# Joining the 16-row inverses of RWKV's time mixing by 32 by 32 products in the array's own tiles

## The chip, the core and the metric

The kernel runs on one core of one Trainium2 chip. The metric is the device time of one execution in microseconds, as the median over several runs of the same program. A profile of one execution stands beside the times; its span runs from the first to the last instruction of the core.

## What is computed

Two layers over all 256 positions at once, everything in float32. Each layer is half a SwiGLU, a mixer, half a SwiGLU:

```python
x = x + 0.5 * swiglu(rms_norm(x, ffn1_norm[l]), ffn1_w_gate_up[l], ffn1_w_down[l])
u = rms_norm(x, mix_norm[l]) @ w_in[l]                 # split: SSD | mLSTM | RWKV-7
x = x + concat(y_ssd, y_mlstm, y_rwkv) @ w_out[l]
x = x + 0.5 * swiglu(rms_norm(x, ffn2_norm[l]), ffn2_w_gate_up[l], ffn2_w_down[l])
```

The change lies in the RWKV-7 part, which the reference writes as a recurrence over time for each of 8 heads of 64:

```python
def step(s, inp):
    r_t, w_t, k_t, v_t, kk_t, a_t = inp
    sa = einsum('bhvk,bhk->bhv', s, -kk_t)
    s = s * w_t + sa[..., None] * (kk_t * a_t) + v_t[..., None] * k_t
    return s, einsum('bhvk,bhk->bhv', s, r_t)
```

The kernel works in chunks of 64 positions. Inside a chunk the values `sa` of all positions solve a triangular system, (I + N) U = R, where N is strictly triangular, 64 by 64. There are 8 heads and 4 chunks, so 32 such matrices in a layer; the kernel needs their inverses.

## The kernel before

**The dense work.** The large products (gate/up, down, `w_in`, `w_out`) run as three passes of 32-bit-rounded matmuls, since every weight and activation is split into a high and a low part. A weight piece of 128 by 1024 numbers is loaded by SyncE's DMA queue (L742 to L766), split by ScalarE (L821) and VectorE (L822), and used by TensorE (L854 to L856 in `mm3`, L1070 and L1073 in `gate_up`).

**What sets the order.** Every operation is first recorded by a `Planner`. It has its own costs for each kind of instruction and for each engine's queue, and picks one instruction after the other: on TensorE the dense work fills what the mixers leave, and work that waits for another engine is put off by a margin as long as something else can go. It also places tiles in a shared store of 22 regions, so a smaller tile can let a weight piece be loaded earlier. Every engine then executes its own list strictly in that order. So a change of a few operations gives other lists on all engines.

**The inverse.** The four 16 by 16 diagonal blocks of each matrix go through DRAM (`dn`, L1333 and L1336) so that all 128 blocks lie one on a partition; VectorE inverts them by substitution (L1359 and L1361, 15 steps). They come back through DRAM (`dg`, `dh`, L1366 to L1375) as block diagonals: `G` holds the inverses and `H` their transposes (the kernel keeps both forms, since the array multiplies by a transpose). In both, row blocks 0 to 63 hold one chunk's matrices and rows 64 to 127 those of the other chunk, 16 matrices in each half, 64 columns each.

Two rounds of joining follow. The first takes the parts of N that join 16 to 32 (`M1`, copied out by L1346, with zeros elsewhere): one product Q of `M1` and `G`, then one of `H` and Q that is taken from `G` and one of Q and `H` that is taken from `H` (each multiplies by the transpose of its first factor). The second takes the parts that join 32 to 64, which stay in `NMv` after the diagonal 32 by 32 blocks have been overwritten with zeros by GpSimd (L1348): a product Q of that part and `G`, and one of Q and `H` that is taken from `H`. Each of these five products is one call of `all_pairs` (L1415): 16 matrices in each of two halves, 32 matmuls of 64 by 64 by 64 in two banks of 16 matmuls each, with the tiles at rows 0 and 64 in turn. Each bank is taken out by one ScalarE copy (L1432, L1441) or one VectorE subtraction (L1436, L1437, L1443) of 128 by 512.

After it, a serial loop over the four chunks (L1482 to L1508) uses `H`, with mLSTM's and SSD's matmuls (L1657, L1663, L1677, L1703, L1800) and dense ones put between its steps.

A float32 matmul of the program appears as two MATMUL rows in the trace, and as two weight loads.

## Time and profile before

| what | value |
|---|---|
| median of three runs | 1283.59 us (1280.87 to 1286.09) |
| the profiled execution | 1280.8 us, its span 1279.1 us |
| TensorE, matmul rows | 1236.7 us busy, 97% |
| VectorE | 894.2 us, 70% |
| ScalarE | 700.3 us, 55% |
| GpSimd | 91.7 us, 7% |
| L1423, the five products | 640 matmul rows in two layers |

The page's first part gives busy time, share of the span and count by engine. The view by windows gives the same for stretches of the span, and the timeline lists an engine's instructions in order, with the idle time before a row and what ended it in brackets. Rows of the same line that follow each other are merged: the first number is the start, the second the time from that start to the end of the last, and x32 the number of instructions. The ends of matmuls are modelled, so in a merged row the last matmul's own duration is to be taken off before the rest is divided among the starts.

### The profile page before, as it was taken

Reading aid. Unit: us, or ns where it says so; the run is one execution under the profiler, and the core shown is the slowest. Engines: PE = TensorE matmul, PEld = TensorE weight load, DVE = VectorE, ACT = ScalarE, POOL = GpSimd, SP = SyncE. Lnnn points to the kernel's source line nnn. Section 1 sums busy time; section 2 is a strip of 40 time slices with the busy share of each in tenths; the row PEclk is TensorE's granted clock in tenths of the full one; section 3 lists DMA queues with packets and bytes.
Section 4 is the critical chain, followed back from the end, with each engine's and each line's share of the span. In section 5 each row is a group of like instructions: output and inputs, shape, how many; then the busy total and the mean of one; then the engine's idle time right before and its main releaser. Section 6 shows DMA issues by size and latency. Waiting matters only on the chain. (4 is left out here: it accounts for less than half of the span.)

```text
span 1279.1 us, 21014 instructions
## 1 busy us (share of the span) xinstructions
PE 1236.7 (97%) x7938; PEld 1067.8 (83%) x7938; DVE 894.2 (70%) x1448; ACT 700.3 (55%) x1233; POOL 91.7 (7%) x153
## 2 busy tenths in 40 slices
PE   7999998989999999999999999999899999999997
PEld 6888887978997888888878888789889888888886
DVE  6766666876599476666676666769766993766664
ACT  7555545647456375555565555565575553655553
POOL 2000002210012010000000000121100220000001
PEclk9999999999999999999999999999999999999999
DMA  9986644035347596655556656610532675966300
GB/s 318 341 267 188 191 116 116 1 87 130 108 143 256 172 311 204 198 186 169 173 165 187 176 183 179 167 48 2 149 92 85 205 255 165 311 198 194 103 1 33
DMA packets 281877, 210.22 MB, mean 164 GB/s; under 512 B 23856, under 2 KB 257200, under 8 KB 281776
## 3 DMA queue, kind: packets, MB, share of 16 engines
q1 hardware_dynamic: 281776, 208.89, 53.9%
q8 instruction: 62, 1.02, 0.3%
q14 instruction: 39, 0.32, 0.1%
HBM read 207.01 MB, written 1.84 MB: 163 GB/s over the span
## 5 line engine op out<-in xcount | busy, mean ns | idle before, releaser
L822 DVE TENSOR_TENSOR region<-region,region 128x1024 fp32r<-128x1024 f32 (+1 forms) x382 | 445.2, 1209 | 76.6 <-ACT region L821 75.1
L1070 PE MATMUL bank<-region,region 128*128 128x512 f32 x1280 | 402.1, 395 | 0.0
L821 ACT ACTIVATE region<-region 128x1024 fp32r<-128x1024 f32 (+1 forms) x382 | 377.9, 1039 | 30.1 <-DMA region<-in_w_in_dram 7.8
L854 PE MATMUL bank<-region,region 128*128 128x512 f32 (+1 forms) x1104 | 385.9, 350 | 6.4 <-DVE region L1190 3.2
L856 PE MATMUL bank<-region,region 128*128 128x512 f32 (+1 forms) x1104 | 383.7, 349 | 3.4 <-DVE region L873 2.9
L855 PE MATMUL bank<-region,region 128*128 128x512 f32 (+1 forms) x1104 | 384.1, 348 | 0.0
L1073 PEld LDWEIGHTS bank<-region,region 128*128 128x128 f32 x1280 | 240.2, 188 | 55.3
L1073 PE MATMUL bank<-region,region 128*128 128x256 f32 x1280 | 252.9, 278 | 0.0
L854 PEld LDWEIGHTS bank<-region,region 128*128 128x128 f32 x1104 | 209.9, 190 | 31.5 <-DVE region L1190 2.6
L856 PEld LDWEIGHTS bank<-region,region 128*128 128x128 f32 x1104 | 209.7, 190 | 30.6 <-DVE region L873 3.8
L855 PEld LDWEIGHTS bank<-region,region 128*128 128x128 f32 x1104 | 210.0, 190 | 23.4 <-issue 1.7
L1070 PEld LDWEIGHTS bank<-region,region 128*128 128x128 f32 x1280 | 200.9, 189 | 6.6 <-DVE region L873 0.3
L1081 ACT ACTIVATE region<-bank 128x256 f32<-128x256 f32 (+1 forms) x84 | 31.0, 374 | 209.4 <-PE bank L1073 209.4
L1083 DVE TENSOR_TENSOR region<-bank,region 128x256 f32<-128x256 f32 (+1 forms) x84 | 34.3, 411 | 117.8 <-ACT region L1081 117.8
L1085 ACT ACTIVATE region<-region 128x256 f32<-128x256 f32 (+1 forms) x84 | 33.9, 407 | 55.8 <-DVE region L1084 55.8
L873 DVE TENSOR_TENSOR region<-region,region 128x256 fp32r<-128x256 f32 (+2 forms) x88 | 36.9, 424 | 37.0 <-ACT region L872 37.0
L872 ACT ACTIVATE region<-region 128x256 fp32r<-128x256 f32 (+2 forms) x88 | 36.2, 417 | 38.8 <-DVE region L1087 38.4
L890 POOL TENSOR_SCALAR smalls<-smalls 128x1 f32<-128x1 f32 x14 | 6.1, 434 | 623.7 <-ACT region L886 623.6
L886 ACT ACTIVATE region<-res 128x512 f32<-128x512 f32 x28 | 17.6, 630 | 53.4 <-DVE res L882 51.4
L1190 DVE SCALAR_TENSOR_TENSOR region<-bank,pv,region 128x255 f32<-128x255 f32 (+2 forms) x84 | 39.9, 479 | 4.7 <-ACT region L1187 2.6
L872 ACT ACTIVATE region<-bank 128x512 fp32r<-128x512 f32 x28 | 16.6, 599 | 41.3 <-PE bank L1202 20.3
L1087 DVE TENSOR_TENSOR region<-region 128x256 f32<-128x256 f32 (+1 forms) x70 | 28.7, 413 | 9.7 <-ACT region L1085 2.6
(303 smaller groups left out, 1026.0 us busy)
## 6 DMA issues: line engine op xcount, KB each, us to landing
region<-in_f_gu_dram SPq DMA_DIRECT2D x352, 256.0 KB, 4.7
region<-in_f_dn_dram SPq DMA_DIRECT2D x88, 512.0 KB, 5.4
region<-in_w_in_dram SPq DMA_DIRECT2D x80, 512.0 KB, 4.6
region<-in_w_out_dram SPq DMA_DIRECT2D x32, 512.0 KB, 4.7
region<-in_prow_dram SPq DMA_DIRECT2D x4, 512.0 KB, 4.3
region<-in_prow_dram SPq DMA_DIRECT2D x6, 256.0 KB, 4.4
region<-in_w_gate_dram SPq DMA_DIRECT2D x2, 512.0 KB, 3.7
dn<-region SPq DMA_DIRECT2D x64, 4.0 KB, 1.5
```

The source lines that it names most:

```text
L821: act.activation(out=hi[:, c], in_=src[:, c], func=AF.Copy)
L822: dve.tensor_tensor(out=lo[:, c], in0=src[:, c], in1=hi[:, c].bitcast(F32), op=ALU.subtract)
L854: pe.matmul(o, lhsT=ah, rhs=bh, start=start, stop=False, skip_group_check=True)
L855: pe.matmul(o, lhsT=ah, rhs=bl, start=False, stop=False, skip_group_check=True)
L856: pe.matmul(o, lhsT=al, rhs=bh, start=False, stop=stop, skip_group_check=True)
L872: act.activation(out=hi, in_=src, func=AF.Copy)
L873: dve.tensor_tensor(out=lo, in0=src, in1=hi.bitcast(F32), op=ALU.subtract)
L1070: pe.matmul(banks[g], lhsT=wh[:, k, g, :], rhs=hT.both(4 * i + k), start=i == k == 0, stop=False, skip_group_check=True)
L1073: pe.matmul(banks[g][:, T:], lhsT=wl[:, k, g, :], rhs=hT(4 * i + k)[0], start=False, stop=i == 1 and k == 3, skip_group_check=True)
L1083: dve.tensor_tensor(out=s[:, ts], in0=gate[:, ts], in1=s[:, ts], op=ALU.add)
L1085: act.activation(out=s[:, ts], in_=s[:, ts], func=AF.Silu)
L1190: dve.scalar_tensor_tensor(out=dst[:, s:T], in0=ps[:, 0:T - s], scalar=col(cw + 3 - s), in1=dst[:, s:T], op0=ALU.mult, op1=ALU.add)
```

## The change

The matrices are no longer kept as 64 by 64 with zeros. `G` now holds the 32 by 32 diagonal blocks alone (32 columns for each of 16 matrices, 512 in place of 1024); so do `M1` and a new `G_` for the transposes. `H` stays 64 wide, and only its lower-left 32 by 32 corner is zeroed.

The first round is three calls of `blocks`: each has 64 matmuls of 32 by 32 by 32, in the four tiles of the array at rows 0, 32, 64 and 96, all into one bank. VectorE subtracts once from `G` (128 by 512) and four times, 32 partitions at a time, into the diagonal blocks of `H`. The second round is two products of 32 matmuls each, only for the one 32 by 32 block that is not zero: the first reads rows 0 to 31 of a half and writes rows 32 to 63, the second goes back. ScalarE takes them out in two copies of 32 partitions each, and the last copy has the factor -1 and writes the corner of `H` that no other operation writes. Since `NMv`'s block is read directly, GpSimd's 8 memsets a layer on it are gone.

So 160 float32 matmuls a layer of 64 by 64 by 64 become 256 of 32 by 32 by 32. The DMAs are as many and as large as before. The loads of two rows of parameters (`lnw`, `lnb`, L1400 and L1401) are recorded as to follow `H`'s writes; `H` is now written by DMA no more, so they wait for its memset alone.

```diff
-            M1 = new(1024)
+            M1 = new(512)
...
-                        act.activation(out=M1n[rr, i * 4:i * 4 + 4, :, d + 16:d + 32],
+                        act.activation(out=M1n[rr, i * 4:i * 4 + 4, :, 16:32],
                                        in_=NMv[i][rr, :, c, :, c0 + d + 16:c0 + d + 32], func=AF.Copy, scale=rmask[rr])
-                        gps.memset(NMv[i][rr, :, c, :, c0 + d:c0 + d + 32], 0.0)
...
-            G, H = (new(1024).rearrange("p (n t) -> p n t", n=16) for i in range(2))
+            G, G_ = (new(512).rearrange("p (n t) -> p n t", n=16) for i in range(2))
+            H = new(1024).rearrange("p (n t) -> p n t", n=16)
             gps.memset(G, 0.0, after=pm)
-            gps.memset(H, 0.0, after=pm)
-            for dst, src in ((G, dg), (H, dh)):
+            gps.memset(G_, 0.0, after=pm)
+            for c in range(2):
+                gps.memset(H[64 * c + 32:64 * c + 64, :, 0:32], 0.0, after=pm)
+            for dst, src in ((G, dg), (G_, dh)):
...
-            def all_pairs(lhs, rhs):
-                for i in range(2):
-                    b = bank()
-                    bv = b.rearrange("p (n t) -> p n t", n=8)
-                    for n in range(8):
-                        for r0 in (0, 64):
-                            q = slice(r0, r0 + 64)
-                            pe.matmul(bv[q, n, :], lhsT=lhs(q, i * 8 + n), rhs=rhs(q, i * 8 + n),
-                                      start=True, stop=True)
-                    yield slice(i * 8, i * 8 + 8), bv
+            def blocks(lhs, rhs):
+                b = bank().rearrange("p (n t) -> p n t", n=16)
+                for n in range(16):
+                    for r0 in range(0, 128, 32):
+                        q = slice(r0, r0 + 32)
+                        pe.matmul(b[q, n, :], lhsT=lhs[q, n, :], rhs=rhs[q, n, :], start=True, stop=True)
+                return b
+            def kept(b, rows=(slice(0, 128),)):
+                v = new(512).rearrange("p (n t) -> p n t", n=16)
+                for q in rows:
+                    act.activation(out=v[q], in_=b[q], func=AF.Copy)
+                return v
...
+            Q = kept(blocks(M1v, G))
+            dG, dH = blocks(G_, Q), blocks(Q, G_)
+            dve.tensor_tensor(out=G, in0=G, in1=dG, op=ALU.subtract)
+            for r0 in range(0, 128, 32):
+                q = slice(r0, r0 + 32)
+                c0 = r0 % 64
+                dve.tensor_tensor(out=H[q, :, c0:c0 + 32], in0=G_[q], in1=dH[q], op=ALU.subtract)
+            first_, second = ([slice(64 * c + d, 64 * c + d + 32) for c in range(2)] for d in (0, 32))
+            b = bank().rearrange("p (n t) -> p n t", n=16)
+            for n in range(16):
+                for c in range(2):
+                    s_, t_ = first_[c], second[c]
+                    pe.matmul(b[t_, n, :],
+                              lhsT=NMv[n // 8][s_, n // 2 % 4, 1 - c, n % 2, 64 * c + 32:64 * c + 64],
+                              rhs=G[s_, n, :], start=True, stop=True)
+            Q = kept(b, second)
+            b = bank().rearrange("p (n t) -> p n t", n=16)
+            for n in range(16):
+                for c in range(2):
+                    s_, t_ = first_[c], second[c]
+                    pe.matmul(b[s_, n, :], lhsT=Q[t_, n, :], rhs=H[t_, n, 32:64], start=True, stop=True)
+            for c in range(2):
+                act.activation(out=H[first_[c], :, 32:64], in_=b[first_[c]], func=AF.Copy, scale=-1.0)
```

The planner makes new lists of it. In the changed kernel's lists L1418 is the matmul of `blocks`, L1442 and L1450 those of the second round, L1424 the copy in `kept`, L1452 the copy into `H`; lines further down stand 9 higher than before (L1469 becomes L1478, L1638 becomes L1647, L1657 becomes L1666), and the loads of `lnw` and `lnb` become L1404 and L1405.

TensorE's list in layer 0, between the first and the second round, before (the matmuls of L1657 are mLSTM's queries and keys, L854 to L856 dense work):

```order
L1423 MATMUL bank_89<-region_395,region_298 64x64 x4
L855 MATMUL bank_88<-region_152,region_2604 128x256
L856 MATMUL bank_88<-region_152,region_2604 128x256
...
L1657 MATMUL bank_87<-region_1954,region_2431 128x256
L1657 MATMUL bank_89<-region_1954,region_2431 128x256
...
L854 MATMUL bank_90<-region_131,region_194 128x256
L855 MATMUL bank_90<-region_131,region_194 128x256
L1423 MATMUL bank_91<-region_642 64x64 x6
```

The same place in the changed kernel:

```order
L1478 MATMUL bank_88<-region_2035,region_298 64x64 x8
L1418 MATMUL bank_87<-region_2035,region_395 32x32 x35
...
L1418 MATMUL bank_88<-region_395,region_2035 32x32 x35
L1442 MATMUL bank_87<-region_448,region_2192 32x32 x16
L1442 MATMUL bank_87<-region_448,region_298 32x32 x16
L1666 MATMUL bank_89<-region_1954,region_2425 128x256
L1666 MATMUL bank_90<-region_1954,region_2425 128x256
...
L1666 MATMUL bank_87<-region_1954,region_2425 128x256
L1450 MATMUL bank_88<-region_837,region_1954 32x32
```

The dense matmuls that stood between the products are gone from here: the second round follows the first directly, and seven of mLSTM's eight matmuls stand right behind its first product.

ScalarE's list at the same place, before (L1432 and L1441 are the copies of `Q`, L1630 an exponential of mLSTM's and SSD's decay, L1638 the Silu whose result L1657 multiplies):

```order
L1432 ACTIVATE region_642<-bank_93 128x512
L1432 ACTIVATE region_642<-bank_91 128x512
...
L1471 ACTIVATE region_448<-bank_89 128x512
...
L606 ACT_TABLE_LOAD
L1638 ACTIVATE region_1954<-region_1954 128x1024
L1742 ACTIVATE region_2487<-region_2487 128x512
L1441 ACTIVATE region_642<-bank_87 128x512
```

And in the changed kernel:

```order
L821 ACTIVATE region_2557<-region_395 128x1024
L1188 ACTIVATE region_2461<-bank_89,pv 128x256
...
L1424 ACTIVATE region_2035<-bank_87 128x512
...
L1480 ACTIVATE region_395<-bank_88 128x512
...
L606 ACT_TABLE_LOAD
L1647 ACTIVATE region_1954<-region_1954 128x1024
L1751 ACTIVATE region_2461<-region_2461 128x512
L1424 ACTIVATE region_1954<-bank_87 32x512 x2
```

The order of the table load, the Silu and the copies of `Q` is as before; one split of a weight piece (L821) now stands ahead of the first copy.

SyncE's list in layer 1, ahead of the stores of the 16 by 16 blocks to DRAM (L1333), before:

```order
L757 DMA region_4322<-in_w_gate_dram 128x1024
L746 DMA region_752<-in_w_in_dram 128x8x128
L746 DMA region_7237<-in_w_in_dram 128x8x128 x2
L746 DMA region_2790<-in_w_in_dram 128x8x128 x2
L746 DMA region_3902<-in_w_in_dram 128x8x128
L746 DMA region_4374<-in_w_in_dram 128x8x128
L746 DMA region_4188<-in_w_in_dram 128x8x128
L1333 DMA dn<-region_7475 16x4x16 x6
```

And in the changed kernel:

```order
L757 DMA region_837<-in_w_gate_dram 128x1024
L746 DMA region_642<-in_w_in_dram 128x8x128
L746 DMA region_448<-in_w_in_dram 128x8x128
L746 DMA region_7336<-in_w_in_dram 128x8x128 x2
L746 DMA region_448<-in_w_in_dram 128x8x128
L746 DMA region_642<-in_w_in_dram 128x8x128
L746 DMA region_4004<-in_w_in_dram 128x8x128
L746 DMA region_752<-in_w_in_dram 128x8x128
L746 DMA region_4004<-in_w_in_dram 128x8x128
L1333 DMA dn<-region_7562 16x4x16 x6
```

Nine weight pieces stand there in place of eight; in layer 0 it is eight in both.

## The prediction

> **What bounds the kernel now.** I read the page's shares first, then the chain, then windows around the two places where the five products stand.

> ```profile
> span 1279.1 us, 21014 instructions
> PE 1236.7 (97%) x7938; PEld 1067.8 (83%) x7938; DVE 894.2 (70%) x1448; ACT 700.3 (55%) x1233; POOL 91.7 (7%) x153
> 275.00:300.00 25.00, 19.22 (x156) 18.43 (x155) 17.54 (x53) 15.70 (x41) 2.90 (x6) 1.00 0.66 191
> 300.00:325.00 25.00, 24.19 (x449) 21.79 (x450) 14.17 (x24) 19.23 (x42) 0.00 (x0) 1.00 0.37 81
> 500.00:600.00 100.00, 100.00 (x532) 85.77 (x531) 66.78 (x98) 52.47 (x85) 0.00 (x0) 1.00 0.60 188
> 900.00:925.00 25.00, 20.31 (x160) 19.54 (x160) 16.19 (x45) 12.94 (x35) 3.99 (x10) 0.98 0.66 184
> 925.00:950.00 25.00, 23.34 (x361) 21.57 (x359) 15.78 (x35) 19.73 (x47) 0.00 (x0) 0.95 0.39 91
> ```

> A window's row gives its length, then busy time and count on TensorE's matmuls, its weight loads, VectorE, ScalarE, GpSimd, and the granted clock. TensorE is the bound: it idles for 42.4 us in the whole span and not at all in the dense stretch 500 to 600. Around the inverse it idles 5.8 and 0.8 us in layer 0, 4.7 and 1.7 us in layer 1. So matmul time saved is saved from the end, unless a wait of TensorE takes its place; time saved elsewhere counts only if TensorE waits for it.

> **The products.** The first two rows are windows of L1423 alone, the others are from the timeline and from groups by form.

> ```profile
> 300.00:330.00 30.00, 10.60 (x320) 9.91 (x320) 1.00 0.47 111
> 935.00:965.00 30.00, 10.79 (x320) 10.11 (x320) 1.00 0.30 70
> L1423 PE MATMUL bank<-region x192: 218/218/267, 314.3 to 325.6; 64*64 64x64 f32 x192
> 314.33 4.00 PE L1423 MATMUL bank<-region 64*64 64x64 f32 x128
> 328.63 0.68 PE L1487 MATMUL bank<-region,region 64*64 64x64 f32 x8
> 321.65 1.89 PE L1657 MATMUL bank<-region,region 128*128 128x256 f32 x8
> 260.93 0.64 PE L1309 MATMUL bank<-region,region 128*32 128x256 f32 x8
> ```

> Now they take 10.60 + 10.79 = 21.4 us. In the longest run a matmul starts every (4.00 - 0.22) / 127 = 29.8 ns, with two tiles in turn, so one every 59.6 ns in a tile. A lone tile of 64 columns (L1487) gives (0.68 - 0.22) / 7 = 66 ns, with L1423's 218 ns for the last; L1657's 256 columns give (1.89 - 0.38) / 7 = 216 ns, 0.38 us being one matmul of that shape, as in L854's row further down. So the pace goes with the columns: 64 more cost about 50 ns, and 32 columns should take some 32 ns in a tile. That four tiles can run at once L1309 shows: eight matmuls of 256 columns in four column tiles end after 0.64 us, where the 216 ns each would make 1.7.

> Per layer the change has 192 matmuls in four tiles (384 rows) and 64 in two tiles (128 rows): 96 rounds of four and 64 of two. At 36 ns each, 32 and a little for the switch between tiles, that is 160 x 36 = 5.8 us; with 0.2 us, the modelled length of a last matmul, for each of six groups, 7.0 us a layer, 14.0 us in both: 7.4 below 21.4.

> One more term lies in this. Every matmul row has a weight load, and the instructions themselves are loaded:

> ```profile
> q8 instruction: 62, 1.02, 0.3%
> DMA to landing us min/median/max: 1.8/2.2/3.4
> ```

> The first row is the page's: 62 packets, 1.02 MB, 0.3% of 16 engines' span. 7938 + 7938 rows of TensorE are 62 times 256, so this is TensorE's list, 256 instructions (128 matmul rows) in a packet, and a packet takes 0.003 x 16 x 1279 / 62 = 1.0 us. The second is the landing time of the small loads of L1375. If the next packet is asked for only when one is used up, 128 rows can't go faster than one such round trip, 2.2 us, 17 ns a row. The old products need 128 x 29.8 ns = 3.8 us a packet and never notice; two `blocks` calls in a row want a packet a microsecond. What is loaded ahead covers the first call, not the second and the third. I take 0.8 us a layer, between nothing and 2 x (2.2 - 1.0) = 2.4. So the products come to 15.6 us, **-5.8**.

> Bounds: if a tile does not get faster below 64 columns (66 ns as L1487's), 96 x 66 + 64 x 66 = 10.6, with 1.2 for the groups 11.8 a layer, 23.6 in all: **+2.2**. If 29.8 ns is not the tiles' pace but the most that matmuls can be handed out at, 512 x 29.8 = 15.3, with 1.2 16.5 a layer, 33.0: **+11.6**. L1309's eight speak against it, but eight may have been queued. The other end is -7.4. I stay near it, since the pace follows the columns in three shapes.

> [...]

> **The waits.** In layer 0 the products now stand in one block on TensorE, and ScalarE and VectorE must follow.

> ```profile
> 309.64 1.78 PE L1423 MATMUL bank<-region,region 64*64 64x64 f32 x52 [0.27 <-ACT region L1471]
> 309.46 1.93 ACT L1630 ACTIVATE region<-bank,region 128x128 f32<-128x128 f32 x7
> 311.21 1.16 ACT L1432 ACTIVATE region<-bank 128x512 f32<-128x512 f32 x2
> 314.20 1.28 ACT L606 ACT_TABLE_LOAD   x1
> 315.50 1.06 ACT L1638 ACTIVATE region<-region 128x1024 f32<-128x1024 f32 x1
> 320.83 1.08 ACT L1441 ACTIVATE region<-bank 128x512 f32<-128x512 f32 x2 [3.75 <-PE bank L1423]
> 317.56 1.27 DVE L1436 TENSOR_TENSOR region<-region,bank 128x512 f32<-128x512 f32 x2
> 947.91 1.84 PE L1423 MATMUL bank<-region,region 64*64 64x64 f32 x54 [0.37 <-ACT region L1630]
> 950.35 2.33 PE L1423 MATMUL bank<-region,region 64*64 64x64 f32 x66 [0.60 <-DVE region L1436]
> ```

> ScalarE's list stays, but for one copy of `Q` in place of two and one split of a weight piece (1.04 us) ahead of it, so `Q` is there at about 311.4. TensorE, whose first product now ends at 309.64 + 1.78 = 311.4 and takes 128 x 9 ns = 1.15 in place of 64 x 29.8 = 1.9, is ready at about 310.6: 0.8 us of wait. Dense matmuls covered this before; they have been moved away. The subtraction from `G` takes 0.64 us after the second product, while the third covers about as much: 0.4 more. Then come seven of L1657's (now L1666), which multiply by the Silu (L1638). It ended at 316.56, and with the table load ahead of it can end at about 316.1: TensorE is there at 315.0, so 1.1. Behind that wait stand the last product's matmuls (L1450) and the serial loop. Sum 2.3, now 0.27. In layer 1, where one of L1657's groups and half of L1469 still stand between the products, I count 1.7 against 0.97. So **+2.7**; the ends are 0 (slower products fill the same time) and 5.4, each wait twice as long.

> **Loads.** In layer 1 a ninth weight piece stands ahead of the stores at L1333.

> ```profile
> 843.42 0.37 SPq L746 DMA_DIRECT2D region<-in_w_in_dram  x1
> 892.87 15.85 SPq L1333 DMA_DIRECT2D dn<-region  x32
> 914.27 1.13 PE L1648 MATMUL bank<-region,region 128*128 128x128 f32 x8 [1.86 <-DMA region<-in_wv_dram]
> 916.43 1.06 ACT L821 ACTIVATE region<-region 128x1024 fp32r<-128x1024 f32 x1 [4.26 <-DMA region<-in_w_in_dram]
> 923.48 0.38 PE L854 MATMUL bank<-region,region 128*128 128x256 f32 x1 [2.41 <-DVE region L1190]
> ```

> SyncE's queue stands empty from 843.8 to 892.9, so the ninth has 49 us to be issued and costs the stores nothing; if its region came free late, all of them and with them the inversion would be late by that much. It gives ScalarE a piece to split in its 4.26 us of idleness, and TensorE dense work in a stretch where it waits 1.86 + 2.41 us. The first wait is for another load and stays, the second hangs on VectorE; I take **-1.0**, between 0 and -4.3.

> **Edits at nothing.** GpSimd's memsets on `NMv` go:

> ```profile
> L1348 POOL MEMSET region<- x16: 301/304/312, 264.9 to 909.8; 32x256 f32 x16
> 299.08 0.38 SPq L1367 DMA_DIRECT2D dh<-region  x1
> 300.38 3.76 SPq L1375 DMA_DIRECT2D region<-dg  x8
> ```

> 4.9 us of an engine that is busy 7%, and `H`'s and `G_`'s memsets are as early as before. VectorE has five subtractions in place of six, ScalarE five copies in place of four, at 0.6 us. The loads of `lnw` and `lnb` go ahead of `dg`'s store; SyncE is idle there, waiting for the inverses, and if not, they cost 2 x 0.4 us on the way to L1375.

> **The sum.** -5.8 + 2.7 - 1.0 = -4.1, so the profiled execution goes from 1280.8 to 1276.7. It lay 2.8 us under the median of the runs shown; with that, 1279.5.

> **The rivals.**
> A, **no faster tiles or longer waits**: 32 columns cost what 64 do. For it: 218 ns as the length of every L1423, and a lone tile's 66 ns where columns alone would give 54. Against it: the paces above. +2.2 + 2.7 - 1.0 = +3.9, or half of it if the tile's time falls half way: 1285.
> B, **the waits don't come**: the Silu and the splits move forward as TensorE does, packets arrive in time, and the dense piece fills layer 1's hole. For it: ScalarE was idle 3.75 us just ahead of L1441, so its list has slack. -7.4 + 0 - 4.3 = -11.7, so 1272.
> C, **the rate of instructions binds**: 1024 matmul rows in place of 640, each with its weight load, at 29.8 ns each. It decides from the point where the four tiles together want one sooner than they can be handed out or loaded: at 17 ns, one packet a round trip, the products would be 512 x 17 = 8.7 + 1.2 a layer, still -1.6; above 18.6 they lose. At 29.8, with no waits left, +11.6 - 1.0 = +10.6: 1294, slower.
> [...]

> **How the numbers follow.** Half a percent, 6.4 us, is about what a measurement of this kernel tells from no change: faster is below 1277.2, slower above 1290.0. The forecast gets 0.46, its own range 1275 to 1284; a third of it (0.15) is below 1277.2, the rest no change. A 0.20: 0.17 no change, 0.03 slower. B 0.22, faster. C 0.12: 0.03 no change, 0.09 slower. So faster 0.37, same 0.51, slower 0.12. The range goes from 1269, a little under B, to 1290, beyond A; C's upper part and the end of B are left out.

> **What would show it.** The products' rows together 15 to 17 us, 1024 of them, with starts of 8 to 10 ns at first and a pause inside the second and third product: right. Steady starts at 16 ns are A, near 30 are C, none slower than 9 is B's first step. TensorE waiting for L1424, for VectorE's subtraction and for L1647 about 2.3 us in layer 0 shows the second term, an idle under 4.3 us in all between 912 and 926 the third. I am wrong if the dense work elsewhere starves through another order of the weight loads, which I have only followed around the inverse.

## The result, and the profile after

The change is slower: 1292.34 us (median of 9 runs, 1288.27 to 1297.06) against 1283.66 (9 runs), a ratio of 1.0061 with a 95% interval of 1.0044 to 1.0077. The forecast was 1279.5, with 1269 to 1290 as the range. Rival C, the rate of instructions, had 1294 and a chance of 0.12.

The first fence is from the page of the changed kernel: span, engines, TensorE's instruction packets.

```profile
span 1290.9 us, 21769 instructions
PE 1239.4 (96%) x8322; PEld 1068.0 (83%) x8322; DVE 896.6 (69%) x1446; ACT 700.5 (54%) x1235; POOL 82.6 (6%) x141
q8 instruction: 65, 1.06, 0.3%
```

384 rows of matmuls and as many weight loads more, 3 packets of 256 more; idle time of TensorE 51.5 us in place of 42.4.

To see where it arose I bounded stretches in both kernels by the same dense matmuls (in order of time the 1409th, 1881st, 4225th and 4815th of L854 to L856, L1070 and L1073), so that each stretch holds one layer's mixers. First before, then the change, then the change's L1418 (first round), L1442 and L1450 (second round) alone.

```profile
278.70:430.40 151.70, 145.38 (x1336) 127.52 (x1337) 120.76 (x212) 89.30 (x161) 14.10 (x16) 1.00 0.58 175
885.60:1061.00 175.40, 167.26 (x1534) 148.63 (x1534) 140.11 (x260) 100.17 (x187) 19.21 (x25) 0.99 0.50 149
```
```profile
281.40:437.00 155.60, 145.40 (x1527) 127.50 (x1528) 121.41 (x211) 89.51 (x162) 11.40 (x12) 0.96 0.56 173
893.70:1072.90 179.20, 166.33 (x1728) 145.78 (x1728) 141.43 (x259) 100.19 (x188) 13.32 (x19) 0.97 0.47 144
...
281.40:437.00 155.60, 5.33 (x384) 4.76 (x384) 0.96 0.56 173
893.70:1072.90 179.20, 4.62 (x384) 4.07 (x384) 0.97 0.47 144
...
281.40:437.00 155.60, 2.22 (x64) 1.95 (x64) 0.96 0.56 173
893.70:1072.90 179.20, 1.21 (x64) 1.10 (x64) 0.97 0.47 144
...
281.40:437.00 155.60, 1.44 (x64) 1.22 (x64) 0.96 0.56 173
893.70:1072.90 179.20, 1.44 (x64) 1.22 (x64) 0.97 0.47 144
```

The two stretches grew from 327.1 to 334.8 us, +7.7. The products fell from 21.39 to 16.26, **-5.1**. TensorE's other work, but for two rows at the edges the same, grew from 312.64 - 21.39 = 291.25 to 311.74 - 16.26 = 295.48, **+4.2**, at a clock of 0.96 and 0.97 in place of 1.00 and 0.99. Idle time grew from 14.46 to 23.06, **+8.6**. The remaining 4.1 of the 11.8 us by which this profiled span is longer lie outside the mixers, where nothing was changed; the medians, 8.7 apart, say that most of that is this one execution's.

The idle time, in the timeline of TensorE, layer 0 and then layer 1:

```profile
312.00 1.27 PE L1418 MATMUL bank<-region,region 32*32 32x32 f32 x126
313.20 1.15 PE L1478 MATMUL bank<-region,region 64*64 64x64 f32 x32
314.64 1.26 PE L1418 MATMUL bank<-region,region 32*32 32x32 f32 x78 [0.29 <-issue]
317.80 1.63 PE L1418 MATMUL bank<-region,region 32*32 32x32 f32 x128 [1.89 <-issue]
321.80 0.79 PE L1418 MATMUL bank<-region,region 32*32 32x32 f32 x41 [2.38 <-issue]
...
325.19 5.03 PE L1666 MATMUL bank<-region,region 128*128 128x256 f32 x14
...
949.55 1.29 PE L1418 MATMUL bank<-region,region 32*32 32x32 f32 x128
950.77 0.85 PE L1478 MATMUL bank<-region,region 64*64 64x64 f32 x21
952.83 0.56 PE L1478 MATMUL bank<-region,region 64*64 64x64 f32 x11 [1.21 <-issue]
...
958.65 1.31 PE L1418 MATMUL bank<-region,region 32*32 32x32 f32 x128 [2.09 <-issue]
962.38 0.64 PE L1418 MATMUL bank<-region,region 32*32 32x32 f32 x29 [2.42 <-issue]
963.43 3.62 PE L1666 MATMUL bank<-region,region 128*128 128x256 f32 x8
```

Three things are to be seen. The tiles are as fast as hoped: 126 rows in 1.27 us, with 0.19 us for the last (1.27 - 0.19) / 125 = 8.6 ns from start to start. But TensorE stops inside a product, where no operand is missing: "issue" is time in which it waits for nothing that the profile shows. And between two such pauses stand exactly 128 rows, which with their weight loads are the 256 instructions of one packet. The pauses of 1.2 us and more, with the smaller 0.29 in layer 0 and 0.23 at the first two rows of L1418, add up to 10.5 us. Then L1666 runs slowly: 14 rows in 5.03 us, with 0.54 (its median length) for the last (5.03 - 0.54) / 13 = 345 ns each, 216 before.

That is the clock (the last number but two of a row):

```profile
315.00:320.00 5.00, 2.53 (x203) 2.29 (x201) 1.15 (x2) 4.70 (x10) 0.00 (x0) 0.85 0.39 122
320.00:325.00 5.00, 2.52 (x113) 2.39 (x114) 2.01 (x4) 0.59 (x1) 0.00 (x0) 0.50 0.01 3
325.00:330.00 5.00, 5.00 (x16) 3.93 (x16) 0.74 (x2) 1.63 (x4) 0.00 (x0) 0.63 0.01 3
960.00:965.00 5.00, 2.62 (x35) 2.29 (x36) 2.31 (x4) 1.18 (x2) 0.00 (x0) 0.52 0.02 3
```

By the trace's own record of the clock the two stretches hold 23.9 us at half clock, against 3.4 before. Of these 17.1 begin among the pauses (at 318.5 and 960.2). The other 6.8 begin at 291.2 and 909.0, ahead of any product, so not all of the +4.2 is the pauses' doing.

### The profile page after: what moved, and what is told of

Same layout as the page of the kernel before. It is cut to its first block, busy times and chain, and to the rows that moved or that the text cites. A ratio compares the mean times of both kernels' runs of the same rounds, so it can differ in the third digit from the quotient of the medians.

```text
span 1290.9 us, 21769 instructions
## 1 busy us (share of the span) xinstructions
PE 1239.4 (96%) x8322; PEld 1068.0 (83%) x8322; DVE 896.6 (69%) x1446; ACT 700.5 (54%) x1235; POOL 82.6 (6%) x141
## 3 DMA queue, kind: packets, MB, share of 16 engines
q8 instruction: 65, 1.06, 0.3%
HBM read 207.01 MB, written 1.84 MB: 162 GB/s over the span
## 4 chain that ended last, share of the span: by engine, by line
PE 84%; DVE 9%; issue 2%; ACT 2%; DMA 2%; SPq 1%; POOL 0%; POOLq 0%; DVEq 0%; ACTq 0%
PE bank L1070 23%; PE bank L854 14%; PE bank L855 14%; PE bank L856 14%; PE bank L1073 11%; DVE region L822 2%; DVE region L1190 1%; PE bank L1666 1%; DMA region<-dn 1%; PE bank L1418 1%; DVE region L1299 1%; PE bank L922 1%; PE bank L1202 1%; PE bank L1809 1%; SPq L1333 1%
## 5 line engine op out<-in xcount | busy, mean ns | idle before, releaser
L1070 PE MATMUL bank<-region,region 128*128 128x512 f32 x1280 | 402.2, 395 | 0.0
L821 ACT ACTIVATE region<-region 128x1024 fp32r<-128x1024 f32 (+1 forms) x382 | 377.9, 1039 | 26.5 <-PE bank L855 15.8
L854 PE MATMUL bank<-region,region 128*128 128x512 f32 (+1 forms) x1104 | 387.4, 352 | 2.6 <-DVE region L1359 1.1
L856 PE MATMUL bank<-region,region 128*128 128x512 f32 (+1 forms) x1104 | 386.2, 351 | 3.4 <-DVE region L873 2.9
L1073 PEld LDWEIGHTS bank<-region,region 128*128 128x128 f32 x1280 | 240.2, 188 | 55.3
L1073 PE MATMUL bank<-region,region 128*128 128x256 f32 x1280 | 252.9, 278 | 0.0
L856 PEld LDWEIGHTS bank<-region,region 128*128 128x128 f32 x1104 | 212.0, 192 | 32.5 <-DVE region L873 3.8
L854 PEld LDWEIGHTS bank<-region,region 128*128 128x128 f32 x1104 | 211.8, 192 | 29.0 <-issue 2.1
L1070 PEld LDWEIGHTS bank<-region,region 128*128 128x128 f32 x1280 | 200.9, 189 | 6.6 <-DVE region L873 0.3
L1190 DVE SCALAR_TENSOR_TENSOR region<-bank,pv,region 128x255 f32<-128x255 f32 (+2 forms) x84 | 40.3, 480 | 5.0 <-ACT region L1187 2.4
```

What stands on the lines that cost most here:

```text
L821: act.activation(out=hi[:, c], in_=src[:, c], func=AF.Copy)
L854: pe.matmul(o, lhsT=ah, rhs=bh, start=start, stop=False, skip_group_check=True)
L856: pe.matmul(o, lhsT=al, rhs=bh, start=False, stop=stop, skip_group_check=True)
L1070: pe.matmul(banks[g], lhsT=wh[:, k, g, :], rhs=hT.both(4 * i + k), start=i == k == 0, stop=False, skip_group_check=True)
L1073: pe.matmul(banks[g][:, T:], lhsT=wl[:, k, g, :], rhs=hT(4 * i + k)[0], start=False, stop=i == 1 and k == 3, skip_group_check=True)
L1190: dve.scalar_tensor_tensor(out=dst[:, s:T], in0=ps[:, 0:T - s], scalar=col(cw + 3 - s), in1=dst[:, s:T], op0=ALU.mult, op1=ALU.add)
```

## The experiments

The theory (P): TensorE's instructions arrive in packets of 256, no faster than one in some 3.7 us (3.73 us from run to run, 958.65 to 962.38 in the change); with little work per instruction TensorE runs dry, and the clock falls behind the pauses. Rivals: small tiles block each other (R); the order of the work, from which the dense matmuls went away, makes the loss (W). Times before are medians of runs on the same chip.

**thrice: is it per call or per instruction?**

```diff
+                for again in range(3):
                     for n in range(16):
                         for r0 in range(0, 128, 32):
```

> The change with each call of blocks issuing its 64 matmuls three times into the same bank (the result does not change): 768 rows more a layer. Theory P: beyond the stock the pace is one packet (128 rows) in 3.7 us, 29 ns a row, as a sawtooth of 1.2 us of rows and 2.5 us of pause: 768 x 29 = 22 us more a layer, about 1292 + 45 = 1337, and more where the clock falls. Rival R: a pause per call, not per row, so 768 x 9 ns = 7 us more a layer: about 1306.

1342.42 us, a single run (before 1283.37). The timeline of TensorE, layer 0:

```profile
326.55 1.94 PE L1419 MATMUL bank<-region,region 32*32 32x32 f32 x128 [0.40 <-issue]
330.00 1.94 PE L1419 MATMUL bank<-region,region 32*32 32x32 f32 x128 [1.51 <-issue]
333.73 1.94 PE L1419 MATMUL bank<-region,region 32*32 32x32 f32 x128 [1.79 <-issue]
337.73 1.94 PE L1419 MATMUL bank<-region,region 32*32 32x32 f32 x128 [2.06 <-issue]
341.46 2.02 PE L1419 MATMUL bank<-region,region 32*32 32x32 f32 x128 [1.78 <-issue]
345.46 0.95 PE L1419 MATMUL bank<-region,region 32*32 32x32 f32 x50 [1.99 <-issue]
```

A sawtooth of 128 rows: five periods from 326.55 to 345.46, 3.78 us each, 29.5 ns a row, although the clock has fallen and a run of 128 now takes 1.94 us in place of 1.3. So the pause does not come with the tiles' own time, and P's number stands. One thing speaks for R still: a pass of 64 matmuls is 128 rows too. But the pauses don't keep to the calls: in the change the first long one comes 78 rows into the second product, and the next one 128 rows later.

The packets' own records in the trace (queue q8) settle it. In thrice the last five transfers ahead of a pause's end were over at 328.58, 332.28, 336.28, 340.08 and 344.05 us, and the runs begin at 330.00, 333.73, 337.73, 341.46 and 345.46, 1.4 to 1.5 us later each time. A transfer takes 0.9 to 1.1 us there, and starts 1.1 to 1.6 us after the run before has begun. In the change all five pauses of over a microsecond end 1.4 to 1.5 us after a transfer (316.41 and 317.80, 320.27 and 321.80 are the first two). TensorE waits for its next packet; R is refuted. The most that it is fed here is 256 instructions in 3.8 us, and the transfer is only 1 us of that.

The old products took 128 x 29.8 = 3.8 us a packet, just at this limit. As far as the traces show, that is chance: a shorter run, the 52 rows at 309.64, has the same pace, (1.78 - 0.22) / 51 = 30.6 ns.

**turned and second_only: fewer instructions.** In turned the third product goes, and VectorE transposes in its place; second_only is the kernel before with the change's second round (and without the memsets on `NMv`).

```diff
# turned, against the change
-            dG, dH = blocks(G_, Q), blocks(Q, G_)
+            dG = blocks(G_, Q)
...
-                dve.tensor_tensor(out=H[q, :, c0:c0 + 32], in0=G_[q], in1=dH[q], op=ALU.subtract)
+                dve.transpose(out=H[q, :, c0:c0 + 32], in_=G[q])
# second_only, against the kernel before
-            for s, b in all_pairs(m2, of(G)):
-                act.activation(out=Qw[:, s], in_=b, func=AF.Copy)
...
+                    pe.matmul(b[t_, n, :],
+                              lhsT=NMv[n // 8][s_, n // 2 % 4, 1 - c, n % 2, 64 * c + 32:64 * c + 64],
+                              rhs=G[s_, n, 0:32], start=True, stop=True)
```

> The change without the third product of the first round: the diagonal blocks of H come from G's by VectorE's 32 by 32 transposes (four of 32x512) in place of 64 matmuls and four subtractions. 384 rows a layer in place of 512, and the one place where two calls of blocks follow each other is gone. Theory P: the pauses that end with 'issue' fall from 10.5 us to 2 to 4, products -1.2 us a layer, clock loss more than halved: about 1279. Rival R: two of three calls are left, so two thirds of the pauses, 7 us, and of the clock loss: about 1286. Rival W: the order is as in the change, waits for ScalarE and VectorE stay, so about 1290.

> The first round as in the kernel before (96 matmuls of 64 by 64 by 64 a layer), the second as in the change (64 of 32 by 32 by 32). 320 matmul rows a layer, as many as before, in place of 512. Theory P (TensorE's instructions arrive 256 at a time, one packet in some 3.7 us, with a small stock): no pause that ends with 'issue' of 2 us, since the 64-wide rows ask for no more than 256 instructions in 3.8 us; the second round's 128 rows at about 17 ns in place of 29.8, so -1.6 us a layer, total about 1280.5. Rival R (four 32-row tiles that write one bank block each other for some 2 us per call, whatever the number of instructions): no call of that kind is left, so the same 1280. Rival W (the loss comes from the new order, in which no dense work stands between the products): the second round still follows the first at once, so half of the loss stays: about 1288.

turned: 1280.53 us, ratio to before 0.9978 (0.9967 to 0.9989). second_only: 1280.30 us, 0.9980 (0.9967 to 0.9993). Waits of TensorE in turned:

```profile
PE bank L1418 <- issue: 6.6, 5, 2.5
...
PE bank L856 <- issue: 1.2, 1, 1.2
```

7.8 us of pauses are left, where I had expected 2 to 4: leaving out 64 matmuls a layer takes away the longest burst, but the two calls that stay are still 256 instructions in a microsecond each. second_only has no such pause at its products (its one row of this kind, 1.1 us, is at L1660). Both times came out near P's, and second_only without W's half of the loss (1288). In turned P's number is in part luck, since its pauses stayed at R's count of 7. Against the change its mixers (279.8 to 431.0 and 888.5 to 1060.7 us) took 11.4 us less: 4.1 in the products, where P had 2.4, 3.4 in idle time, where P had over 6, and 3.9 in the other work, whose growth is gone but for 0.3.

**pause: what does idle time do to the clock?** The kernel before, the same lists, but ScalarE copies the first half of `Q` nine times in each round (`again` gives 8 for these two copies, 0 for all else).

```diff
+            for _ in range(self.again(op)):
+                call_from(op.line, op.call, ...)
             call_from(op.line, op.call, ...)
```

> The kernel before with the same order on every engine, but ScalarE makes the first copy of Q nine times in each round (the same values into the same place), so that TensorE has to wait some 2 us twice a layer, with no small tile and no instruction of TensorE more: about +8 us of idle time in both layers. Theory K (the granted clock falls because TensorE idles): half clock for at least 10 us more than the 3.4 of before, and the matmuls behind the pauses longer, so +12, about 1295. Rival S (the clock falls because of the small tiles themselves): half clock as before, only the idle time is added, about 1291.

1304.34 us, ratio 1.0188 (1.0163 to 1.0213). Windows around the products, before and then pause:

```profile
310.00:340.00 30.00, 29.85 (x493) 27.34 (x491) 15.37 (x25) 16.09 (x33) 0.00 (x0) 1.00 0.35 99
940.00:965.00 25.00, 23.91 (x440) 21.70 (x440) 11.47 (x18) 16.21 (x35) 0.00 (x0) 1.00 0.30 78
```
```profile
310.00:340.00 30.00, 20.32 (x344) 18.35 (x341) 10.05 (x16) 19.74 (x35) 0.00 (x0) 0.83 0.22 62
955.00:980.00 25.00, 17.56 (x322) 15.98 (x323) 10.12 (x16) 20.41 (x41) 0.00 (x0) 0.86 0.24 68
```

The pauses came out longer than planned (four of 3.5 to 5.0 us; idle time in the two mixers 29.7 us against 14.5, because the Silu and mLSTM's matmuls became late too), so the total is off. But the question is answered: without one small tile and with no instruction more, the clock in these windows falls from 1.00 to 0.83 and 0.86. Idle time of this length is enough to bring it. The change's pauses are about half as long, and what share of its +4.2 the tiles have is not separated by this. A caution on the label: one wait of 3.5 us in pause is put down to "issue" although it ends just where ScalarE's ninefold copy does (961.1 us), and no packet had ended in the 2 us before. The word alone proves nothing; the 128 rows between two pauses and the packets' records do.

**narrow and wide_turned: half the instructions.** In both the first round has two products of 32 matmuls with 64-row tiles, H's diagonal comes from transposes, and the second round is the change's. In narrow `G` and `Q` are 32 wide; wide_turned is second_only without its third product.

```diff
# narrow, against the change
-                    for r0 in range(0, 128, 32):
-                        q = slice(r0, r0 + 32)
+                    for r0 in (0, 64):
+                        q = slice(r0, r0 + 64)
# wide_turned, against second_only
-            dHs = list(all_pairs(of(Qv), of(H)))
...
+                dve.transpose(out=H[q, :, c0:c0 + 32], in_=G[q, :, c0:c0 + 32])
```

> First round with 64-row tiles but 32 columns: M1 and H are 64 wide with zeros as before, G and Q 32 wide, two products of 32 matmuls, H's diagonal blocks from G's by VectorE's transposes; second round as in the change. 256 rows a layer in place of 512. Theory P: no call asks for more than one packet, no pause that ends with 'issue' over 0.5 us, rows at 16 to 18 ns: 256 x 17 = 4.4 us plus 0.8 for the ends, 5.2 a layer against 10.7 before: -11 us with waits for ScalarE and VectorE of +3: about 1276. Rival R: no four-tile call, the same. Rival W: +8 us of waits stay: about 1281 or more.

> First round with the old 64 by 64 tiles, but without its third product: H's diagonal blocks from G's by VectorE's transposes; second round as in the change. 256 rows a layer, as in the kernel called narrow, half of the change's 512. Theory P (only instructions per time matter): no pause that ends with 'issue' over 0.5 us, products 128 x 29.8 + 128 x 17 = 6.0 us a layer against 10.5 before, 8.8 us less in both, some waits of +3: about 1277. Rival W (once TensorE's work there is short, waits for ScalarE, VectorE and the half clock take its place, whatever the instructions, as in narrow): 1284 or more.

narrow: 1299.92 us, ratio 1.0139 (1.0123 to 1.0155). wide_turned: 1281.98 us, 1.0002 (0.9984 to 1.0020). The first is far off what P said, the second lies with W. The pauses that end with "issue" are 0.7 us at narrow's products, up to 314.78, where ScalarE's copy of `Q` has just ended (314.69), and none in wide_turned; P is right in that, and wrong that it alone decides. wide_turned's products take 14.1 us in place of 21.4, yet its mixers last 326.9 us, as long as before: in layer 0 no dense matmul stands between its products, idle time grew by 2.8 us and the other work by 4.3. narrow's layer 1 takes 10 us more than before's: its serial loop stands almost alone on TensorE and waits five times for VectorE and ScalarE, and the granted clock is at half for 17 us in each of its stretches. Why its list turned out so much worse than wide_turned's I have not settled.

narrow also prices a tile that is 64 by 64 but has only 32 columns to stream:

```profile
311.80 2.25 PE L1416 MATMUL bank<-region,region 64*64 64x32 f32 x64
...
321.44 1.20 PE L1440 MATMUL bank<-region,region 32*32 32x32 f32 x64
```

(2.25 - 0.22) / 63 = 32 ns a row, no better than 29.8 for 64 columns, while 32 by 32 tiles in two rows of tiles take (1.20 - 0.19) / 63 = 16 ns. So it was the smaller tile that halved the time, not the fewer columns.

**The same instructions in other orders.** The planner's constant MARGIN is 1600 in place of 2000 in three kernels: the kernel before (as a control), turned (turned_spread), and the change (after_spread), which also reckons 58 ns for a row pair of small tiles. second_cost and wide_turned_cost reckon that alone.

```diff
-    MARGIN = 2000.0
+    MARGIN = 1600
...
+                    if nn <= 32 and m <= 32:
+                        op.occ = 116
```

> The kernel before with one constant of the planner changed (MARGIN 1600 in place of 2000), as a control: how far another order alone moves the time with the old products. Theory P says nothing of it; if order alone is worth 10 us (rival W), it shows here: within 1283 +- 4 if orders matter little, 10 us off if they matter as much as the change did.

> The change with all its 512 rows a layer, but the planner reckons 58 ns for a row pair of the small tiles (the pace of one packet of instructions) and MARGIN 1600, which puts 12 and 10 dense matmuls and L1478's sixteen between the first product and the other two, 6 behind these. The second and the third product still follow each other, 256 rows. Theory P: the pauses that end with 'issue' fall from 10.5 us to some 6, half clock with them, about 1286. If small tiles as such cost the time, or the waits, it stays at 1292.

> The kernel called turned (H's diagonal blocks by VectorE's transposes, 384 rows a layer) with MARGIN 1600, whose list has 12 and 30 dense matmuls around the second product in layer 0, 17 and 6 in layer 1. The same instructions as in turned, spread. Theory P: a packet's 256 instructions now take 3 to 4 us, pauses that end with 'issue' fall from 7.8 to under 3 us: about 1275. Rival W: as turned, 1280, or worse.

> The kernel called second_only (old first round, small tiles in the second alone) with 58 ns per row pair in the planner's reckoning; its list has dense matmuls between all products of both layers. Theory P: no pause that ends with 'issue' over 0.5 us, as in second_only, so 1280, a little less if its waits of 1 us at the products go. Rival W: the order decides, so 5 us or more off.

> The kernel called wide_turned (256 rows a layer: old tiles in the first round without its third product, small tiles in the second) with 58 ns per row pair of the small tiles in the planner's reckoning, whose list has 49 and 48 dense matmuls between the products. Theory P: no pause that ends with 'issue', and with dense work in the gaps the 8 us of products saved come through where wide_turned lost them to waits and half clock: about 1276. Rival W (what is saved there returns as a wait elsewhere, since the stretch hangs on ScalarE's and VectorE's chain): as wide_turned, 1282.

| kernel | rows a layer | "issue" at the products, us | median, us | ratio to before (95%) |
|---|---|---|---|---|
| before_m1600 | 320 | 0 | 1287.17 | 1.0029 (1.0015 to 1.0042) |
| after_spread | 512 | 5.7 | 1289.65 | 1.0049 (1.0035 to 1.0063) |
| turned_spread | 384 | 2.1 | 1284.36 | 1.0009 (0.9994 to 1.0025) |
| second_cost | 320 | 0 | 1277.92 | 0.9957 (0.9942 to 0.9973) |
| wide_turned_cost | 256 | 0 | 1285.89 | 1.0022 (1.0005 to 1.0039) |

The pauses come from rows of this kind, after_spread, turned_spread:

```profile
PE bank L1420 <- issue: 5.7, 2, 3.2
```
```profile
PE bank L1418 <- issue: 1.7, 1, 1.7
PE bank L1478 <- issue: 0.4, 1, 0.4
```

With the same instructions and other work between the bursts the pauses shrink as P said, 10.5 to 5.7 and 7.8 to 2.1. The times don't follow as well: MARGIN 1600 alone costs 3.8 us. Against that control the small tiles cost 2.5 us in after_spread (whose list also has the 58 ns) and bring 2.8 in turned_spread. So W is right in its way: by their ratios to before, these five moved by 1.5 to 4 us, up or down, against the same products in the first order. In wide_turned_cost the dense matmuls do stand between the products, and the serial loop behind them in layer 0 has none left: TensorE waits there for VectorE and ScalarE (1.64, 0.68, 1.35 and 0.68 us), and the clock stands at half from 339.6 to 346.4. The dense work is a limited stock; what it covers at one place it leaves bare at another.

second_cost is faster than both kernels, by 0.4% against the one before: only the second round has small tiles, and no instruction was added. In this order dense work stands between the first product and the next two, and between the two of the second round, though not between all, as I had written. Its interval overlaps second_only's, so what the order gave is not shown.

## Why the prediction was wrong

- **The products**: -5.8 with packets, -7.4 without; their rows measured -5.1. The paces held: 8.6 ns a row in four tiles (8 to 9 taken), 16 in two. The reason I gave, that the pace goes with the columns streamed, is refuted by narrow's 64x32 rows.
- **The packets: the step that failed.** The term was in the sum, with the right unit (128 rows), as 0.8 us a layer between 0 and 2.4. It measured 10.5 / 2 = 5.2. I had taken a small load's landing, 2.2 us, as the upper end of a packet's round trip; thrice shows 3.8, with the transfer itself only 1 us of it. With 3.8 my own bound would have read 2 x (3.8 - 1.0) = 5.6. What was loaded ahead covered the first call in layer 1 (128 rows without a pause) and the 21 rows of L1478 behind it, not the second and the third, as I had said. The longest run of small rows without a pause was 227 (after_spread, at 311.07); how much could be held is not shown.
- **Rival C** was this mechanism at 29.8 ns a row, priced at +10.6. The mechanism is what happened, and thrice has 29.5 ns a row for it. The price is not: rows and pauses together came to -5.1 + 10.5 = +5.4, where C had +11.6, since not every row had to wait for a packet. That the total came near C's 1294 is in part luck, for C had no clock in it. What spoke against it, L1309's eight quick starts, fits into what is already loaded: eight rows are 16 instructions of 256. I had the packet row on the table and computed the limit from the wrong one. The before trace did not show it: its longest run used up a packet in just 3.8 us.
- **The waits**, +2.7: at the products only 0.68 us of them came, for L1424, against 1.24 before. The pauses had swallowed them, as C said ("no waits left").
- **The loads**, -1.0: apart from the pauses layer 1 idles 12.9 - 5.7 = 7.2 us, as before without its waits at the products (8.1 - 1.0). The hole at 914 to 923 closed, and one of 2.19 us opened at 908 (L1586). Nothing was gained.
- **The clock** was missing: no term said what a lower clock does to the work around the products. That work grew by 4.2 us; most of the half clock stands among the pauses, some ahead of the products.

## What to carry to other kernels

When a matmul is made smaller, count instructions per microsecond beside the time of a tile: here 128 matmul rows with their weight loads cannot go by in less than 3.8 us for long. Smaller tiles paid here, by 0.2 to 0.4%, only with about as many rows as before (second_only, second_cost, turned). With 512 rows the pauses and the clock took the gain, also in after_spread with half the pauses; with 256 other waits and the clock did (wide_turned, narrow). Look in the trace of before for the busiest stretch and see whether it stands just at that limit already. And a pause on TensorE can cost more than itself: among those of 1.9 to 2.4 us in the change the clock fell to half for 10.2 and 6.8 us. It need not: before, a wait of 3.0 us that ended at 286.8 was followed by full clock.

## What the runs showed of the hardware

```profile
318.71 2.91 DVE L1433 STREAM_TRANSPOSE region<-region 32x512 f32<-32x512 f32 x4
```
- The clock falls to 0.83 to 0.86 over 25 to 30 us around pauses of 3.5 to 5.0 us on TensorE, without a small tile (pause).
